# Hybrid decoder trunk in split f32: the places of matrix operands within 256 bytes of SBUF, and queries and keys computed with the weights stationary

## The chip, the cores and the metric

The kernel runs on one core of a Trainium2 chip. The metric is the device time in microseconds (us) of one execution. Three executions of the kernel before took 1136.25, 1136.45 and 1136.63 us, so the median is 1136.45 us. The profiled execution took 1136.86 us; the span from its first to its last instruction is 1135.1 us, so 1.76 us lie around the span.

## The reference

One sequence of 256 tokens with 2048 features passes one layer, all in f32:

```
h = rms_norm(x, norm1_g);  proj = h @ w_in                    # 2048 x 6152
q_a, k_a, v_a, f_a, q_b, k_b, v_b = split(proj)               # 8 + 8 heads of 128; f_a: 8 columns
y_a = forgetting attention(q_a, k_a, v_a, log_sigmoid(f_a + forget_b))
y_b = dilated attention(q_b, k_b, v_b, rel_bias)              # three dilations, mixed by their softmax sums
x = x + concat(rms_norm(y_a), rms_norm(y_b)) @ w_out          # 2048 x 2048
h = rms_norm(x, norm2_g)
x = x + square(relu(h @ w_mlp_in)) @ w_mlp_out                # 2048 x 8192, 8192 x 2048
out = rms_norm(x, final_norm_g)
```

## The kernel before, in words

**Products.** Every f32 matrix is held as two `float32r` parts, hi and lo, and each product is three: hi by hi, lo by hi, hi by lo. A matrix product on TensorE (PE) has a stationary operand of 128 by 128, which a weight load (LDWEIGHTS, the row PEld) brings in, and a moving operand that is streamed past it. The profile names a product `acc<-moving,stationary`.

**Chunks, steps, slots.** The weights are taken in chunks of 512 columns, in the order in which they run: for each of four groups of four heads `q`, `v`, `k` (16 feature tiles each), eight chunks `o` of `w_out` (8 tiles each), then four rounds of four chunks `u` (`w_mlp_in`) and four chunks `d` (`w_mlp_out`) of 16 tiles. A slot is one feature tile of 128 rows (`kt`), a step is two slots. SP loads the raw weights of two steps in one DMA. `split` (L144) makes the parts of a step three steps ahead: ScalarE (ACT) writes `whi` (L168), VectorE (DVE) writes `wlo` (L169). There are four buffers of each, so ACT starts on a step's `whi` when PE has done with the one four steps earlier.

**Two forms.** In the plain form (`product`, L295: q, k, v, o, d) the activations are stationary and 512 weight columns move: six products a slot. In the turned form (`turned_product`, L303: only u) the weights are stationary, in four blocks of 128 columns, and 256 tokens move: twelve products a slot. The plain form leaves tokens on the partitions, the turned form features.

**Accumulators.** A chunk has two PSUM tiles `acc`; the pool holds four, so a chunk needs the two that were freed by the chunk before the last. What empties them, and all the attention work, is tied to slots by `at(slot, function)` and written out behind that slot's products (`run_side`). Each engine works through its instructions in that written order.

**Queries and keys.** `drain_qk` empties q and k into `nat`, ACT one half, DVE the other, and scales rows by the norm of their token. `turn_qk` then turns each pair of heads with four PE transposes (L463) and splits the result from PSUM. `e` is the last slot of the chunk: drain at `e` (for the first chunk at `e + 3`), turning at `e + 2` and `e + 3`. Of the k chunk's attention, the last head's `values` comes at `e + 29`, which is slot `e + 13` of the next q chunk, and `group_norm` of the second group at `e + 31`, slot `e + 15` of the next q chunk.

**Places.** The start of a tile in a partition of SBUF, modulo 256 bytes, follows from the order and sizes of the tiles in the pools. By the addresses in the built programs it is:

| tile | before | after |
|---|---|---|
| `aT_hi`, `aT_lo` (normed x, features on partitions): stationary for q, k, v; moving for u | 224 | 32 |
| `big_hi`, `big_lo` (attention output, later the MLP's hidden state): stationary for o, d | 160 | 32 |
| `whi`, `wlo` where they move | 160 | 32 |
| `whi`, `wlo` where they are stationary | 160 | 224 |
| `q`, `v` parts: stationary in the attention | 224 | 0 |
| `k` and `p` (probability) parts: moving in the attention | 32 | 0 |

Rows of these tiles and the buffers of a pool are multiples of 256 bytes long, so each operand of a group starts at the same place. In the last d chunk the parts of its first four steps go into `aT_hi` and `aT_lo`, which are free then; there the moving operand starts at 224.

Of the kernel before, what the change touches and what calls it, by code (L numbers as in the profile page):

```python
# [19 lines left out]
P = 128  # L20
D_MODEL = 2048
SEQ = 256
# [15 lines left out]

LEAD = 3
WARM, WARM2 = 8, 1  # L40


def _constants():
    i = np.arange(P)
    upto = (i[:, None] <= i[None, :]).astype(np.float32)
    after = (i[:, None] > i[None, :]).astype(np.float32)
    tri = np.where(i[None, :] <= i[:, None], 0.0, NEG).astype(np.float32)
    head = (i[:, None] % 32 == np.arange(NH)[None, :]).astype(np.float32)
    pack = np.concatenate([after, -upto, tri, np.zeros((P, P), np.float32), tri, head], axis=1)
# [19 lines left out]
def kernel(  # L69
# [21 lines left out]
    w_in, w_out, w_up, w_down = w_in[0], w_out[0], w_mlp_in[0], w_mlp_out[0]  # L91

    one = ctx.enter_context(tc.tile_pool(name="one", bufs=1))
    two = ctx.enter_context(tc.tile_pool(name="two", bufs=2))
    wraw = ctx.enter_context(tc.tile_pool(name="wraw", bufs=4))
    wsplit = ctx.enter_context(tc.tile_pool(name="wsplit", bufs=LEAD + 1))
    psum = ctx.enter_context(tc.tile_pool(name="psum", bufs=2, space=PSUM))
    dram = ctx.enter_context(tc.tile_pool(name="dram", bufs=1, space=DRAM))
# [45 lines left out]
    def split(i, j0=0, n=2):  # L144
# [31 lines left out]
    warm = zeros[:, :CW // 2].bitcast(BF16)  # L176
    half_t = one.tile([P, TB], F32, name="half_t")
    ones = one.tile([P, 1], F32, name="ones")
    nc.vector.memset(zeros[:, :CW // 2], 0.0)
# [14 lines left out]
    for c in range(1, 4):  # L194
        load_x(4 * c, 4 * c + 4)
        load(2 * c)
    fb = one.tile([P, NH], F32, name="fb")
    relx = one.tile([N_BUCKETS + 1, NH], F32, name="relx")
    nc.vector.memset(relx, 1.0)
    pk = one.tile([P, 5 * P + NH], F32, name="pk")  # L200
    pick_sb = two.tile([P, RW], F32, name="pr")[:N_BUCKETS + 1]
# [8 lines left out]

    mcat = pk[:, 2 * P:5 * P]
    head = pk[:, 5 * P:]
    gcat = one.tile([P, TB, P], F32R, name="gcat")
# [8 lines left out]
    nc.scalar.activation(ones, ones, AF.Copy)  # L222
    gT = one.tile([P, 48], F32, name="gT")

# [30 lines left out]
    def rsqrt(dst, ssq, n):  # L255

        w = dst.shape[1]
        v = two.tile([P, TB], F32, name="rs_v")[:, :w]
        t = two.tile([P, TB], F32, name="rs_t")[:, :w]
# [7 lines left out]
    ssq1 = one.tile([P, TB, 4], F32, name="ssq1")  # L267
    ssq1s = one.tile([P, TB], F32, name="ssq1s")
    rstd1 = one.tile([P, TB], F32, name="rstd1")
    rstdq = one.tile([P, TB], F32, name="rstdq")  # L270

# [8 lines left out]
    def first_norm():  # L280
        nc.vector.tensor_reduce(ssq1s, ssq1, axis=mybir.AxisListType.X, op=ALU.add)
        rsqrt(rstd1, ssq1s, D_MODEL)
        nc.vector.tensor_scalar(rstdq, rstd1, QSCALE, None, op0=ALU.mult)

# [57 lines left out]

    logf = one.tile([P, TB, NH], F32, name="logf")
    lf_hi, lf_lo = (
# [12 lines left out]
    def forget_gates():  # L357
        f = psum.tile([P, 512], F32, name="tr")
        for t in range(TB):
            nc.tensor.transpose(f[:, 2 * t * NH:2 * (t + 1) * NH], fTs[0][:, t * P:(t + 1) * P], ident[:2 * NH, :2 * NH])  # L360
        z = one.tile([P, TB, NH], F32, name="fz")
        e = one.tile([P, TB, NH], F32, name="fe")
        u = one.tile([P, TB, NH], F32, name="fu")
        d = one.tile([P, TB, NH], F32, name="fd")
        n = one.tile([P, TB, NH], F32, name="fn")
        for t in range(TB):
# [76 lines left out]

    nat = {}

    def drain_qk(g, what, ci):
        acc = accs.pop(ci)
        scale = rstdq if what == "q" else rstd1
        ts = [two.tile([P, CW], F32, name="nat") for _ in range(TB)]
        nc.scalar.activation(ts[0], acc[0], AF.Copy, scale=scale[:, 0:1])  # L450
        nc.vector.tensor_scalar(ts[1], acc[1], scale[:, 1:2], None, op0=ALU.mult)
        nat[g, what] = ts

    def turn_qk(g, what, hp):
        ts = nat[g, what]
        if hp == 0:
# [7 lines left out]
        split_psum(  # L464
            th[:, 2 * hp:2 * hp + 2, :].rearrange("p h s -> p (h s)"),
            tl[:, 2 * hp:2 * hp + 2, :].rearrange("p h s -> p (h s)"), p,
        )
# [3 lines left out]
    def decay_of(hd):  # L471
        decay[hd] = two.tile([P, SEQ], F32R, name="gate_h")
        nc.gpsimd.tensor_scalar(
# [5 lines left out]
    def scores(g, h):  # L479
# [19 lines left out]
        pr = two.tile([P, 3 * P], F32, name="pr")  # L499
        st = two.tile([P, 3, TB], F32, name="st")  # L500
        for t, c0, c1 in spans:
            add = mcat[:, c0:c1] if kind == 0 else relT[:, hd, SEQ - (c1 - c0):]
            nc.vector.tensor_tensor_reduce(  # L503
# [25 lines left out]
    def values(g, h):  # L529
# [12 lines left out]
        first = seen[kind] == 0  # L542
        s = sq[kind] if first else two.tile([P, SEQ], F32, name="sqt")
        nc.scalar.activation(s, y[:, :SEQ], AF.Square)
# [4 lines left out]

    rstdo = [one.tile([P, TB], F32, name=f"rstdo{k}") for k in range(2)]  # L550

# [6 lines left out]

    ssq2 = one.tile([P, TB, 4], F32, name="ssq2")
    ssq2s = one.tile([P, TB], F32, name="ssq2s")  # L560
    rstd2 = one.tile([P, TB], F32, name="rstd2")
    rstd2sq = one.tile([P, TB], F32, name="rstd2sq")

# [30 lines left out]
    gf = relT.rearrange("p h s -> p (h s)")  # L594
    ssq3 = one.tile([P, TB, 5], F32, name="ssq3")
    ssq3s = one.tile([P, TB], F32, name="ssq3s")
    rstd3 = one.tile([P, TB], F32, name="rstd3")

# [31 lines left out]
    def finish(t, n, cs):  # L630
        r, s = rstd3[:, t:t + 1], ssq3s[:, t:t + 1]
        v = two.tile([P, 1], F32, name="fi_v")
        u = two.tile([P, 1], F32, name="fi_u")
        ru = two.tile([P, 1], F32, name="fi_ru")
        nc.vector.tensor_scalar(v, ssq3[:, t, n:n + 1], s, 1.0 / D_MODEL, op0=ALU.add, op1=ALU.mult)
# [39 lines left out]
    for ci, (what, key, *_rest) in enumerate(chunks[:-1]):  # L675
# [107 lines left out]
```

## Time and profile before

| what | value |
|---|---|
| median of three executions | 1136.45 us |
| profiled execution, its span | 1136.86 us, 1135.1 us |
| PE busy | 1124.0 us, 99% of the span |
| PE weight loads busy | 988.8 us, 87% |
| DVE, ACT, POOL busy | 56%, 46%, 3% |
| granted TensorE clock | 0.998 of full speed |
| HBM | 183 GB/s over the span |

Matmuls are pipelined: the profile's duration of one overlaps the next, so the cost of a product is read from the distance between starts, in the timeline or in the chain of waits, and not from its duration. The idle times of DVE and ACT cost nothing by themselves.

### The profile page before, as it was taken

The page shows a single profiled execution, that of the slowest core. Times are in us where ns is not written, and L with a number is a line of the kernel's source. Part 1 is how long each engine was busy: PE and PEld are TensorE (multiplying, and loading weights), DVE is VectorE, ACT ScalarE, POOL GpSimd, SP SyncE. Part 2 cuts the span into 40 slices and gives each one's busy share as a digit, 9 for nine tenths or more (in the row PEclk, how much of TensorE's full clock was granted, in tenths as well). Part 3 has the DMA queues.
Part 4 walks back from the last instruction along what each step waited for, and adds up shares of the span by engine and source line. Part 5 has one row for each costly group of instructions (what it writes and reads, how often), then busy time and mean ns, then how long its engine had stood idle before and what let it go on. Part 6 is the DMA issues. An engine that isn't in the chain of part 4 may idle for free.

```text
span 1135.1 us, 16038 instructions
## 1 busy us (share of the span) xinstructions
PE 1124.0 (99%) x6635; PEld 988.8 (87%) x6635; DVE 639.7 (56%) x795; ACT 521.9 (46%) x675; POOL 31.7 (3%) x57
## 2 busy tenths in 40 slices
PE   9999999999999999999999999999999999999996
PEld 6778888888888889998889998889998889999886
DVE  5665656556566665555555555545555554555564
ACT  5545545545445554454334444343544433454451
POOL 0100200100001000000000000000000000000000
PEclk9999999999999999999999999999999999999999
DMA  8655454454545556556555655566465566556642
GB/s 312 224 183 183 154 185 149 149 185 149 186 156 178 155 179 192 187 179 212 196 185 164 208 186 188 200 199 192 152 220 187 186 193 192 187 171 206 240 148 74
DMA packets 104933, 209.15 MB, mean 184 GB/s; under 512 B 3651, under 2 KB 4508, under 8 KB 104732
## 3 DMA queue, kind: packets, MB, share of 16 engines
q1 hardware_dynamic: 104556, 207.06, 55.8%
q0 software_dynamic: 304, 1.06, 0.3%
q8 instruction: 52, 0.85, 0.3%
q14 instruction: 21, 0.17, 0.0%
HBM read 206.00 MB, written 2.11 MB: 183 GB/s over the span
## 4 chain that ended last, share of the span: by engine, by line
PE 98%; DMA 1%; DVE 0%; SPq 0%; ACT 0%; POOL 0%; issue 0%; DVEq 0%
PE acc L313 32%; PE acc L299 21%; PE acc L301 21%; PE acc L300 21%; PE sc L493 1%; PE sc L538 1%; PE tr L463 1%; DMA raw<-in_w_in_dram 1%; PE tr L250 1%; PE tr L520 0%; PE sc L333 0%; PE sc L490 0%; DVE wlo L169 0%; ACT whi L168 0%; DVE xs L646 0%; SPq L185 0%
## 5 line engine op out<-in xcount | busy, mean ns | idle before, releaser
L169 DVE TENSOR_TENSOR wlo<-raw,whi 128x1024 fp32r<-128x1024 f32 (+1 forms) x381 | 464.1, 1224 | 374.4 <-ACT whi L168 371.6
L168 ACT ACTIVATE whi<-raw 128x1024 fp32r<-128x1024 f32 (+1 forms) x381 | 399.8, 1055 | 404.2 <-PE acc L300 241.4
L313 PE MATMUL acc<-aT_hi,whi 128*128 128x256 f32 x1024 | 287.2, 280 | 0.0
L313 PE MATMUL acc<-aT_hi,wlo 128*128 128x256 f32 x1024 | 286.1, 279 | 0.0
L313 PE MATMUL acc<-aT_lo,whi 128*128 128x256 f32 x1024 | 286.0, 279 | 0.0
L299 PE MATMUL acc<-whi,big_hi 128*128 128x512 f32 (+1 forms) x632 | 246.0, 389 | 0.0
L301 PE MATMUL acc<-wlo,big_hi 128*128 128x512 f32 (+1 forms) x632 | 244.7, 387 | 0.0
L300 PE MATMUL acc<-whi,big_lo 128*128 128x512 f32 (+1 forms) x632 | 244.5, 387 | 0.0
L313 PEld LDWEIGHTS acc<-aT_hi,wlo 128*128 128x128 f32 x1024 | 192.8, 188 | 0.0
L313 PEld LDWEIGHTS acc<-aT_hi,whi 128*128 128x128 f32 x1024 | 192.3, 188 | 0.2
L313 PEld LDWEIGHTS acc<-aT_lo,whi 128*128 128x128 f32 x1024 | 191.6, 187 | 0.2
L299 PE MATMUL acc<-whi,aT_hi 128*128 128x512 f32 x384 | 157.0, 409 | 0.0
L300 PE MATMUL acc<-whi,aT_lo 128*128 128x512 f32 x384 | 152.5, 397 | 0.0
L301 PE MATMUL acc<-wlo,aT_hi 128*128 128x512 f32 x384 | 152.3, 397 | 0.0
L301 PEld LDWEIGHTS acc<-wlo,big_hi 128*128 128x128 f32 x632 | 118.7, 188 | 24.4
L300 PEld LDWEIGHTS acc<-whi,big_lo 128*128 128x128 f32 x632 | 118.8, 188 | 23.4
L299 PEld LDWEIGHTS acc<-whi,big_hi 128*128 128x128 f32 x632 | 118.8, 188 | 22.9
L301 PEld LDWEIGHTS acc<-wlo,aT_hi 128*128 128x128 f32 x384 | 72.5, 189 | 17.4
L299 PEld LDWEIGHTS acc<-whi,aT_hi 128*128 128x128 f32 x384 | 72.7, 189 | 15.3 <-issue 0.6
L300 PEld LDWEIGHTS acc<-whi,aT_lo 128*128 128x128 f32 x384 | 72.7, 189 | 14.0 <-DVE aT_lo L240 0.2
L237 DVE TENSOR_TENSOR big_lo<-nat,big_hi 128x512 fp32r<-128x512 f32 x32 | 22.2, 693 | 22.3 <-ACT big_hi L236 22.3
L507 ACT ACTIVATE pr<-neg,st 128x128 f32<-128x128 f32 (+1 forms) x32 | 14.3, 448 | 40.8 <-DVE st L503 40.8
(160 smaller groups left out, 533.7 us busy)
## 6 DMA issues: line engine op xcount, KB each, us to landing
raw<-in_w_mlp_in_dram SPq DMA_DIRECT2D x64, 1024.0 KB, 5.3
raw<-in_w_mlp_out_dram SPq DMA_DIRECT2D x64, 1024.0 KB, 5.2
raw<-in_w_in_dram SPq DMA_DIRECT2D x42, 1024.0 KB, 5.2
raw<-in_w_out_dram SPq DMA_DIRECT2D x16, 1024.0 KB, 5.1
raw<-in_w_in_dram SPq DMA_DIRECT2D x4, 1040.0 KB, 5.3
raw<-in_w_in_dram SPq DMA_DIRECT2D x3, 512.0 KB, 8.6
xs<-in_x_dram SPq DMA_DIRECT2D x3, 512.0 KB, 9.6
big_lo<-rel_d POOLq DMA_DIRECT2D x1, 1024.0 KB, 7.3
```

Source lines behind the costliest of these rows:

```text
L168: nc.scalar.activation(hi, t, AF.Copy)
L169: nc.vector.tensor_tensor(lo, t, hi.bitcast(F32), op=ALU.subtract)
L237: nc.vector.tensor_tensor(lo, src, hi.bitcast(F32), op=ALU.subtract)
L250: nc.tensor.transpose(p[:, j * SEQ + t * P:j * SEQ + (t + 1) * P], xs[:, t, c:c + P], ident)
L299: nc.tensor.matmul(acc, xh, hi[:, j, cols], start=go, stop=False)
L300: nc.tensor.matmul(acc, xl, hi[:, j, cols], start=False, stop=False)
L301: nc.tensor.matmul(acc, xh, lo[:, j, cols], start=False, stop=end)
L313: nc.tensor.matmul(acc, w[:, j, b * P:(b + 1) * P], a[:, kt, :], start=kt == 0 and b % 2 == 0 and n == 0, stop=kt == kts - 1 and n == 2, s ...
L463: nc.tensor.transpose(p[:, j * SEQ + t * P:j * SEQ + (t + 1) * P], ts[t][:, h * P:(h + 1) * P], ident)
L493: nc.tensor.matmul(s[:, c0:c1], q[:, h, t * P:(t + 1) * P], k[:, h, :c1 - c0], start=n == 0 and kind == 1, stop=n == 2,)
L507: nc.scalar.activation(pr[:, c0:c1], neg[:, c0:c1], AF.Exp, bias=st[:, 0, t:t + 1], scale=-1.0, accum_out=st[:, 1, t:t + 1],)
L538: nc.tensor.matmul(y[:, o0:SEQ], v[:, t, h * P:(h + 1) * P], p[:, c0:c1], start=t == 0 and n == 0, stop=t == 1 and n == 2,)
```

## The change

Three things are changed.

The first is where tiles start. The pools are re-sorted (`lead_in`, `wide`, `few` are new), the parts of the weights get a buffer 256 bytes longer and start at 32 bytes in it where they move, or at 224 where they are stationary, and a tile of 32 bytes ahead of `aT_hi` puts all of `aT` and `big` at 32. To make room one zero block of the mask goes, and `gate_h` and `sqt` have one buffer in place of two.

The second is the form of q and k: they use the turned form, so they arrive with features on the partitions and the transposes go. Their scale now varies along the free axis, so a tile `rows1` with the tokens' factors on all partitions is made once, at slot 19, by two small DVE instructions and one f32 product (L465 of the new kernel). Each half of a chunk is emptied by one DVE instruction from PSUM (L474), then split from SBUF.

The third is when: queries are emptied at `e + 14` and `e + 15`, keys at `e` and `e + 1`.

```diff
+LINE, NEAR, FAR = 64, 8, 56
+TURNED = "qku"
...
-            hi, lo = (wsplit.tile([P, 2, CW], F32R, name=n) for n in ("whi", "wlo"))
+            b = FAR if chunks[ci][0] in TURNED else NEAR
+            hi, lo = (
+                wsplit.tile([P, 2 * CW + LINE], F32R, name=n)[:, b:b + 2 * CW].rearrange("p (j c) -> p j c", j=2)
+                for n in ("whi", "wlo")
+            )
...
-    aT_hi = one.tile([P, KT, SEQ], F32R, name="aT_hi")
-    aT_lo = one.tile([P, KT, SEQ], F32R, name="aT_lo")
+    wide.tile([P, NEAR], F32, name="ahead")
+    aT_hi = wide.tile([P, KT, SEQ], F32R, name="aT_hi")
+    aT_lo = wide.tile([P, KT, SEQ], F32R, name="aT_lo")
...
-        if what == "u":
+        if what in TURNED:
             return turned_product(ci, i, j, kt, kts)
...
-    yT_hi = one.tile([P, 2 * NH, SEQ], F32R, name="big_hi")
-    yT_lo = one.tile([P, 2 * NH, SEQ], F32R, name="big_lo")
+    yT_hi = wide.tile([P, 2 * NH, SEQ], F32R, name="big_hi")
+    yT_lo = wide.tile([P, 2 * NH, SEQ], F32R, name="big_lo")
...
+    def first_norm_rows():
+        d = two.tile([P, CW], F32, name="nat")
+        square = d[:, SEQ:SEQ + P]
+        nc.gpsimd.memset(square, 1.0)
+        p = psum.tile([P, 512], F32, name="tr")
+        for t in range(TB):
+            nc.vector.tensor_scalar(d[:, t * P:(t + 1) * P], ident, rstd1[:, t:t + 1], None, op0=ALU.mult)
+        nc.tensor.matmul(p[:, :SEQ], square, d[:, :SEQ], start=True, stop=True)
+        nc.scalar.activation(rows1, p[:, :SEQ], AF.Copy)
+
+    def drain_qk(g, what, ci, half):
+        if half == 0:
             qkv[g, what] = [one.tile([P, 4, SEQ], F32R, name=what + n) for n in ("_hi", "_lo")]
         th, tl = qkv[g, what]
-        p = psum.tile([P, 512], F32, name="tr")
-        for j in range(2):
-            for t in range(TB):
-                h = 2 * hp + j
-                nc.tensor.transpose(p[:, j * SEQ + t * P:j * SEQ + (t + 1) * P], ts[t][:, h * P:(h + 1) * P], ident)
+        acc = accs[ci][half]
+        n = two.tile([P, CW], F32, name="nat")
+        nc.vector.scalar_tensor_tensor(
+            n.rearrange("p (h s) -> p h s", h=2), acc.rearrange("p (h s) -> p h s", h=2),
+            QSCALE if what == "q" else 1.0, rows1[:, None, :].to_broadcast([P, 2, SEQ]),
+            op0=ALU.mult, op1=ALU.mult,
+        )
         split_psum(
...
-            late = 3 if ci == 0 else 0
-            at(e + late, drain_qk, key, what, ci)
-            at(e + late + 2, turn_qk, key, what, 0)
-            at(e + late + 3, turn_qk, key, what, 1)
+            late = 14 if what == "q" else 0
+            at(e + late, drain_qk, key, what, ci, 0)
+            at(e + late + 1, drain_qk, key, what, ci, 1)
...
+    at(19, first_norm_rows)
```

On PE, around an eviction of queries and keys before, the transposes stand between plain products. Here the scores of one head (L493) end, and the two turnings of a q chunk (L463) follow among the v chunk's products:

```order
L493 MATMUL sc<-k_hi,q_lo 128x256
L463 MATMUL tr<-ident,nat 128x128 x4
L299 MATMUL acc<-whi,aT_hi 128x512
L300 MATMUL acc<-whi,aT_lo 128x512
L301 MATMUL acc<-wlo,aT_hi 128x512
L299 MATMUL acc<-whi,aT_hi 128x512
L300 MATMUL acc<-whi,aT_lo 128x512
L301 MATMUL acc<-wlo,aT_hi 128x512
L463 MATMUL tr<-ident,nat 128x128 x4
```

In the changed kernel there is no such row. This is PE where the third group's v chunk ends (L310 to L312, plain) and its k chunk begins (L324, turned, one row a product); L570 belongs to `group_norm`:

```order
L570 MATMUL tr<-ones,sq_140 128x1 x2
L310 MATMUL acc<-whi,aT_hi 128x512
L311 MATMUL acc<-whi,aT_lo 128x512
L312 MATMUL acc<-wlo,aT_hi 128x512
L310 MATMUL acc<-whi,aT_hi 128x512
L311 MATMUL acc<-whi,aT_lo 128x512
L312 MATMUL acc<-wlo,aT_hi 128x512
L324 MATMUL acc<-aT_hi,whi 128x256
L324 MATMUL acc<-aT_lo,whi 128x256
L324 MATMUL acc<-aT_hi,wlo 128x256
```

The first L324 writes the accumulator of the q chunk's first half, the seventh that of its second half; each waits until DVE has emptied it.

The third place is DVE at the same point. Before, from the last values of the second group (`big_lo`) to the third group's v chunk being emptied (`v_lo`), with the five small instructions of `group_norm` (`rs_v`, `rs_t`, `rstdo`) between:

```order
L240 SCALAR_TENSOR_TENSOR big_lo<-sc,gT,big_hi 128x256
L169 TENSOR_TENSOR wlo<-raw,whi 128x1024
L260 TENSOR_SCALAR rs_v<-tr 128x2
L262 TENSOR_TENSOR rs_t<-rstdo_132 128x2
L263 TENSOR_TENSOR rs_t<-rs_t,rs_v 128x2
L264 TENSOR_SCALAR rs_t<-rs_t 128x2
L265 TENSOR_TENSOR rstdo_132<-rstdo_132,rs_t 128x2
L240 SCALAR_TENSOR_TENSOR v_lo<-acc,rstd_117,v_hi 128x512 x2
```

And after:

```order
L253 SCALAR_TENSOR_TENSOR big_lo<-sc,gT,big_hi 128x256
L474 SCALAR_TENSOR_TENSOR nat<-acc,rows_139 128x512
L250 TENSOR_TENSOR q_lo<-nat,q_hi 128x512
L181 TENSOR_TENSOR wlo<-raw,whi 128x1024
L273 TENSOR_SCALAR rs_v<-tr 128x2
L275 TENSOR_TENSOR rs_t<-rstdo_142 128x2
L276 TENSOR_TENSOR rs_t<-rs_t,rs_v 128x2
L277 TENSOR_SCALAR rs_t<-rs_t 128x2
L278 TENSOR_TENSOR rstdo_142<-rstdo_142,rs_t 128x2
L474 SCALAR_TENSOR_TENSOR nat<-acc,rows_139 128x512
L250 TENSOR_TENSOR q_lo<-nat,q_hi 128x512
L253 SCALAR_TENSOR_TENSOR v_lo<-acc,rstd_127,v_hi 128x512 x2
```

The two evictions of queries (L474) moved in here; the second stands behind a weight split and the group's norm. On ACT the first half's `q_hi` stands ahead of the next `whi`.

## Rows read from the trace of the kernel before

**Rows 1.** The page: span, busy times, and the chain that ended last.
```profile
span 1135.1 us, 16038 instructions
PE 1124.0 (99%) x6635; PEld 988.8 (87%) x6635; DVE 639.7 (56%) x795; ACT 521.9 (46%) x675; POOL 31.7 (3%) x57
PE 98%; DMA 1%; DVE 0%; SPq 0%; ACT 0%; POOL 0%; issue 0%; DVEq 0%
```

**Rows 2.** Chain of waits by time: start, us, what; first d round, second u round.
```profile
506.14 0.24 PE acc L299
593.22 90.45 PE acc L313 x768
683.67 0.24 PE acc L299
```

**Rows 3.** Timeline, PE (start, duration, instruction): fourth group's v chunk.
```profile
300.05 0.40 PE L299 MATMUL acc<-whi,aT_hi 128*128 128x512 f32 x1
...
315.45 0.40 PE L299 MATMUL acc<-whi,aT_hi 128*128 128x512 f32 x1
```

**Rows 4.** Timeline, PE: end of the last chunk, 256 columns moving.
```profile
1120.61 0.28 PE L299 MATMUL acc<-aT_hi,big_hi 128*128 128x256 f32 x1
...
1123.44 0.29 PE L299 MATMUL acc<-whi,big_hi 128*128 128x256 f32 x1
...
1125.96 0.28 PE L299 MATMUL acc<-whi,big_hi 128*128 128x256 f32 x1
```

**Rows 5.** Timeline, PE: values of two heads, first and fourth product.
```profile
282.59 0.28 PE L538 MATMUL sc<-p_hi,v_hi 128*128 128x256 f32 x1
...
282.93 0.22 PE L538 MATMUL sc<-p_hi,v_hi 128*128 128x128 f32 x1
...
343.15 0.28 PE L538 MATMUL sc<-p_hi,v_hi 128*128 128x256 f32 x1
...
343.51 0.22 PE L538 MATMUL sc<-p_hi,v_hi 128*128 128x128 f32 x1
```

**Rows 6.** Chain of waits by time: one turning of two heads.
```profile
89.67 0.44 PE tr L463 x4
```

**Rows 7.** Timeline, PE: the f32 product of 384 columns, and the next.
```profile
68.62 0.81 PE L416 MATMUL sc<-pr,relx 33*8 33x384 f32 x2
69.36 0.50 PE L299 MATMUL acc<-whi,aT_hi 128*128 128x512 f32 x1
```

**Rows 8.** Timeline: second group, last values, to the k chunk's first product.
```profile
136.94 0.38 ACT L544 ACTIVATE sqt<-sc 128x256 f32<-128x256 f32 x1 [1.26 <-PE sc L538]
137.73 0.48 DVE L240 SCALAR_TENSOR_TENSOR big_lo<-sc,gT,big_hi 128x256 fp32r<-128x256 f32 x1 [0.78 <-ACT big_hi L239]
140.94 0.39 PE L299 MATMUL acc<-whi,aT_hi 128*128 128x512 f32 x1
```

**Rows 9.** Timeline: the same in the third group, with `group_norm`.
```profile
214.34 0.48 DVE L240 SCALAR_TENSOR_TENSOR big_lo<-sc,gT,big_hi 128x256 fp32r<-128x256 f32 x1 [0.78 <-ACT big_hi L239]
216.95 0.15 DVE L260 TENSOR_SCALAR rs_v<-tr 128x2 f32<-128x2 f32 x1
217.19 0.73 POOL L261 TENSOR_TENSOR rstdo<-rs_v,half_t 128x2 f32<-128x2 f32 x1 [2.37 <-DVE rs_v L260]
218.00 0.40 PE L299 MATMUL acc<-whi,aT_hi 128*128 128x512 f32 x1
218.55 0.16 DVE L265 TENSOR_TENSOR rstdo<-rstdo,rs_t 128x2 f32<-128x2 f32 x1
```

**Rows 10.** Groups by line: names, shapes, count | busy us, mean ns | idle before.
```profile
L169 DVE TENSOR_TENSOR wlo<-raw,whi 128x1024 fp32r<-128x1024 f32 (+1 forms) x381 | 464.1, 1224 | 374.4 <-ACT whi L168 371.6
L168 ACT ACTIVATE whi<-raw 128x1024 fp32r<-128x1024 f32 (+1 forms) x381 | 399.8, 1055 | 404.2 <-PE acc L300 241.4 <-PE acc L313 154.8 <-DMA raw<-in_w_in_dram 4.6
L236 ACT ACTIVATE big_hi<-nat 128x512 fp32r<-128x512 f32 x32 | 20.2, 632 | 26.1 <-DVE nat L587 26.1
L568 DVE SCALAR_TENSOR_TENSOR xs<-acc,rstdo,xs 128x512 f32<-128x512 f32 x16 | 11.3, 745 | 0.0
```

More of the change, by code (lines that the diff above doesn't have):

```diff
@@ L48, in _constants @@
     head = (i[:, None] % 32 == np.arange(NH)[None, :]).astype(np.float32)
-    pack = np.concatenate([after, -upto, tri, np.zeros((P, P), np.float32), tri, head], axis=1)
+    pack = np.concatenate([after, -upto, np.zeros((P, P), np.float32), tri, head], axis=1)
     dist = np.arange(RW) - 127
@@ L176 @@
     warm = zeros[:, :CW // 2].bitcast(BF16)
-    half_t = one.tile([P, TB], F32, name="half_t")
-    ones = one.tile([P, 1], F32, name="ones")
+    half_t = few.tile([P, TB], F32, name="half_t")
+    ones = few.tile([P, 1], F32, name="ones")
     nc.vector.memset(zeros[:, :CW // 2], 0.0)
@@ L196 @@
         load(2 * c)
-    fb = one.tile([P, NH], F32, name="fb")
-    relx = one.tile([N_BUCKETS + 1, NH], F32, name="relx")
+    fb = few.tile([P, NH], F32, name="fb")
+    relx = few.tile([N_BUCKETS + 1, NH], F32, name="relx")
     nc.vector.memset(relx, 1.0)
-    pk = one.tile([P, 5 * P + NH], F32, name="pk")
+    pk = few.tile([P, 4 * P + NH], F32, name="pk")
     pick_sb = two.tile([P, RW], F32, name="pr")[:N_BUCKETS + 1]
@@ L222 @@
     nc.scalar.activation(ones, ones, AF.Copy)
-    gT = one.tile([P, 48], F32, name="gT")
+    gT = lead_in.tile([P, 96], F32, name="gT")[:, :48]
     def gains(k0, k1):
@@ L257, in rsqrt @@
         w = dst.shape[1]
-        v = two.tile([P, TB], F32, name="rs_v")[:, :w]
-        t = two.tile([P, TB], F32, name="rs_t")[:, :w]
+        v = few.tile([P, TB], F32, name="rs_v", bufs=2)[:, :w]
+        t = few.tile([P, TB], F32, name="rs_t", bufs=2)[:, :w]
         nc.vector.tensor_scalar(v, ssq, 1.0 / n, EPS, op0=ALU.mult, op1=ALU.add)
@@ L265, in rsqrt @@
         nc.vector.tensor_tensor(dst, dst, t, op=ALU.mult)
[L267 to L270, printed above, removed]
+    ssq1 = few.tile([P, TB, 4], F32, name="ssq1")
+    ssq1s = few.tile([P, TB], F32, name="ssq1s")
+    rstd1 = few.tile([P, TB], F32, name="rstd1")
     def first_squares(t, c):
@@ L282, in first_norm @@
         rsqrt(rstd1, ssq1s, D_MODEL)
-        nc.vector.tensor_scalar(rstdq, rstd1, QSCALE, None, op0=ALU.mult)
     accs = {}
@@ L340, in at @@
         side.setdefault(i, []).append((f, a))
-    logf = one.tile([P, TB, NH], F32, name="logf")
+    logf = few.tile([P, TB, NH], F32, name="logf")
     lf_hi, lf_lo = (
@@ L360, in forget_gates @@
             nc.tensor.transpose(f[:, 2 * t * NH:2 * (t + 1) * NH], fTs[0][:, t * P:(t + 1) * P], ident[:2 * NH, :2 * NH])
[L361 to L365, printed above, removed]
+        z = few.tile([P, TB, NH], F32, name="fz")
+        e = few.tile([P, TB, NH], F32, name="fe")
+        u = few.tile([P, TB, NH], F32, name="fu")
+        d = few.tile([P, TB, NH], F32, name="fd")
+        n = few.tile([P, TB, NH], F32, name="fn")
         for t in range(TB):
@@ L442, in drain_v @@
         qkv[g, "v"] = (vh, vl)
[L444 to L456, printed above, removed]
+    rows1 = one.tile([P, SEQ], F32, name="rows1")
+    def first_norm_rows():
[9 more added lines that the diff above has]
+        if half == 0:
             qkv[g, what] = [one.tile([P, 4, SEQ], F32R, name=what + n) for n in ("_hi", "_lo")]
         th, tl = qkv[g, what]
-        p = psum.tile([P, 512], F32, name="tr")
-        for j in range(2):
-            for t in range(TB):
-                h = 2 * hp + j
-                nc.tensor.transpose(p[:, j * SEQ + t * P:j * SEQ + (t + 1) * P], ts[t][:, h * P:(h + 1) * P], ident)
+        acc = accs[ci][half]
[5 more added lines that the diff above has]
+        )
         split_psum(
-            th[:, 2 * hp:2 * hp + 2, :].rearrange("p h s -> p (h s)"),
-            tl[:, 2 * hp:2 * hp + 2, :].rearrange("p h s -> p (h s)"), p,
+            th[:, 2 * half:2 * half + 2, :].rearrange("p h s -> p (h s)"),
+            tl[:, 2 * half:2 * half + 2, :].rearrange("p h s -> p (h s)"), n,
         )
@@ L471, in decay_of @@
     def decay_of(hd):
-        decay[hd] = two.tile([P, SEQ], F32R, name="gate_h")
+        decay[hd] = two.tile([P, SEQ], F32R, name="gate_h", bufs=1)
         nc.gpsimd.tensor_scalar(
@@ L542, in values @@
         first = seen[kind] == 0
-        s = sq[kind] if first else two.tile([P, SEQ], F32, name="sqt")
+        s = sq[kind] if first else two.tile([P, SEQ], F32, name="sqt", bufs=1)
         nc.scalar.activation(s, y[:, :SEQ], AF.Square)
@@ L548, in values @@
         seen[kind] += 1
-    rstdo = [one.tile([P, TB], F32, name=f"rstdo{k}") for k in range(2)]
+    rstdo = [few.tile([P, TB], F32, name=f"rstdo{k}") for k in range(2)]
     def group_norm(kind):
@@ L557, in group_norm @@
         rsqrt(rstdo[kind], p[:, :TB], D_GRP)
[L559 to L562, printed above, removed]
+    ssq2 = few.tile([P, TB, 4], F32, name="ssq2")
+    ssq2s = few.tile([P, TB], F32, name="ssq2s")
+    rstd2 = few.tile([P, TB], F32, name="rstd2")
+    rstd2sq = few.tile([P, TB], F32, name="rstd2sq")
     def drain_o(kind, c, ci):
@@ L594 @@
     gf = relT.rearrange("p h s -> p (h s)")
-    ssq3 = one.tile([P, TB, 5], F32, name="ssq3")
-    ssq3s = one.tile([P, TB], F32, name="ssq3s")
-    rstd3 = one.tile([P, TB], F32, name="rstd3")
+    ssq3 = few.tile([P, TB, 5], F32, name="ssq3")
+    ssq3s = few.tile([P, TB], F32, name="ssq3s")
+    rstd3 = few.tile([P, TB], F32, name="rstd3")
     def load_gf():
```

17 lines of the change are left out of this document (10 added, 7 removed).

## The prediction

> **What bounds the kernel now.** I read the page's busy times and its chain first. The reader is to see that TensorE (PE) is busy for 99% of the span and holds 98% of the chain that ended last, while DVE and ACT are half idle [rows 1]. So the time is a sum of PE's products, and a change is worth what it does to their number, to the distance between their starts, and to PE's waits. Next I read distances, in the chain by time and in PE's timeline.
>
> - Turned products of u: 768 in 90.45 us, 0.1178 us each [rows 2].
> - Plain products of d: from 506.14 to 593.22 there are 384, 0.2268 us each [rows 2].
> - Plain products of q, k and v: from 300.05 to 315.45 there are 66, 0.2333 us each [rows 3].
>
> The last two have one shape, but stand 6.5 ns apart. What differs is where their operands start in a line of 256 bytes: moving and stationary at 160 and 160 in d, at 160 and 224 in q, k, v. The last chunk shows it inside one stage and over one stationary tile: 24 products of 256 columns with the moving operand at 224 take 2.83 us, 0.1179 each, and the next 21 with it at 160 take 2.52 us, 0.1200 each [rows 4]. So places do matter, by some per cent.
>
> The Trainium skill speaks against this: its page "TensorE: Matmul & The Clock Gate", section "Step-by-step: what each phase is for", says that PE has two independent read ports into SBUF, and that loading the next weights takes no read bandwidth from the running product. By that rule places are free and the sum is that of the third rival below; the trace does not agree, since rows 4 differ by 2.1 ns at one shape.
>
> **The change part by part.** All sums are against the profiled execution, 1136.86 us (span 1135.1 us and 1.76 us around it); the median of the runs is 0.41 us below it, and I take that off at the end.
>
> *Transposes.* One turning of two heads is four transposes, 0.44 us in the chain [rows 6]. Eight chunks of q and k have two each, so 16 x 0.44 = 7.0 us go. They lie on PE, with nothing beside them.
>
> *The row factors.* One f32 product of 256 columns is added. The trace's f32 product of 384 columns took 0.74 us to the next start [rows 7], so this is 0.74 x 256/384 = 0.5 us. The two DVE instructions that feed it come a whole chunk before their result is used; if DVE is late there, PE waits some tenths of a us once.
>
> *q and k turned.* 768 plain products become 1536 turned ones with moving and stationary at 32 and 224. In the attention before, products of 256 columns stand at just these places. Three of them in a row take 0.34 us in one head and 0.36 us in another [rows 5]; the sixteen such triples lie between these two and average 0.346 us, 0.1153 each. Bounds are 0.113 and 0.120; I take 0.1153, the mean at the same places and width. 1536 x 0.1153 = 177.1 us replace 768 x 0.2333 = 179.2 us: -2.1 us.
>
> *u.* The same places and products: 3072 x (0.1153 - 0.1178) = -7.7 us.
>
> *v, o, d.* All become 32 and 32. No row has that for 512 columns. Nearest is d with 160 and 160, equal places too, at 0.2268. The largest difference that places make between rows of 512 columns is 6.5 ns, so I bound it by 0.2203 and 0.2333. With the moving operand at 32 the 256-column triples are 2 to 5 ns below those with it at 224 or 160 [rows 4, 5], so I lean below d and take 0.225. v has 384 products: 384 x (0.225 - 0.2333) = -3.2 us. o and d have 1848 that stream `whi` or `wlo` at full width: 1848 x (0.225 - 0.2268) = -3.3 us.
>
> *The evictions.* They leave ACT one copy less and give DVE one instruction more a chunk; both are half idle [rows 1], and their waits cost nothing as long as PE has its operands. Late queries change that. A k chunk writes the accumulators of the q chunk before it. Their second half is emptied at e + 15 and the k chunk begins at e + 17, two slots or 2.8 us later. In the second group DVE comes to it like this, with the mean durations by line [rows 10]: `big_lo` of the last values ends at 138.21 [rows 8]; first half emptied, 0.745, at 138.96; ACT's `q_hi`, 0.632, at 139.6; only then ACT's next `whi`, which stands behind it, 1.055, at 140.65; DVE's `wlo`, 1.224, at 141.9; second half, 0.745, at 142.6, with handovers some 142.7. PE's seventh product of the k chunk wants it at 140.94 [rows 8] + 6 x 0.118 = 141.65, or 141.5 with v faster. So PE waits 1.2 us, with every product behind it. The fourth group has the same queue: 1.2 us. In the third, `group_norm` stands ahead of the second half: `big_lo` ends at 214.82, and the same steps bring `wlo` to 218.5; from `rs_v` to the last `rstdo`, with POOL between, took 216.95 to 218.71, 1.76 us [rows 9]; so 220.25, and the eviction ends at 221.0, with handovers 221.1. PE wants it at 218.00 + 0.7 - 0.15 = 218.55: a wait of 2.5 us. The first group has no attention before it, and there the second half is emptied in time. Together +4.9 us, between 0 and 7. The weights are split three steps (8 us) ahead, so these waits go no further.
>
> *At no cost.* The single buffers of `gate_h` and `sqt` are used once in four slots, and POOL is 3% busy [rows 1]. SP issues the same weight loads in the same order; nothing is moved past a queue.
>
> Sum: -7.0 + 0.5 - 2.1 - 7.7 - 3.2 - 3.3 + 4.9 = -17.9 us, so 1119.0 for a profiled execution and **1118.5 us** for the median.
>
> **The rivals.**
>
> *Streams at 32 are faster than I take them.* If equal places at 32 reach the lower bound, 0.2203, v gives -5.0 and o and d -12.0 in place of -3.2 and -3.3: 1108 us; turned products at 0.113 as well would give 1097. For it: the best triples are at 0.113. Against: they are short sequences.
>
> *Only the distance between the two places counts.* It is 0 in d before and in all plain products after, and 64 in u before (224 and 160) and in the turned ones after (32 and 224, modulo 256). Then u, o and d stay, v falls to 0.2268 (-2.5), q and k cost 1536 x 0.1178 - 179.2 = +1.7, and -7.0 + 0.5 + 4.9 remain: -2.4, so 1134 us. For it: the change keeps both distances. Against: the attention at distance 64 averages 0.1153, not 0.1178.
>
> *Places do nothing; the stage does.* The slower rate of q, k, v would come from the attention and its traffic. Then only +1.7, -7.0, +0.5 and +4.9 count: 1136.5 us, no change. For it: rows 2 and 3 are of different stages. Against: rows 4. This is the time that the skill's two ports would give.
>
> *Slower: 32 with 32 is a bad pair.* If plain products there stand 0.2333 apart, as those of q, k, v do now, o and d cost 1848 x 0.0065 = 12.0 us more, v nothing less, and with turned products left at 0.1178 the sum is +12.1: 1148.5 us. It decides from a plain distance of 0.2279 on if turned products gain nothing, from 0.2330 on if they gain what I take. For it: no row shows the pair. Against: of the two plain pairs in rows 2 and 3 the one with equal places is the faster.
>
> **How the numbers follow.** The forecast has 52%, faster streams 17%, distance alone 16%, stage alone 7%, the bad pair 8%. The forecast's own range is 1110 to 1127, from turned products 2 ns either way. The range of 8 in 10 takes in most of the faster streams at its low end, and the two cases without a gain at its high end: 1103 to 1137 us. A measurement of this kernel can tell 0.2%, 2.3 us, from no change. Faster by more: the forecast (51), faster streams (17), over half of distance alone (9), 1 of the others: 78%. Within: 13%. Slower: 9%, the bad pair and late evictions on top of no gain.
>
> **What would show it.** In the profile after, each u round of 768 products should take 88.5 us in place of 90.45 and each d round 86.4 in place of 87.1; the v products should stand about 0.225 apart. No L463 should be left, and L324 should count 4608 products. At the start of the second, third and fourth k chunk PE should wait some 1.2, 2.5 and 1.2 us for DVE's L474, seven products in. Rounds of u and d with unchanged lengths would mean distance or stage; d rounds at 89 us and more would mean the bad pair. What makes the prediction wrong above all is the distance of plain products at 32 and 32, since each ns of it is 2.2 us.

## The result and the profile after

Four executions of the changed kernel took 1129.44 to 1132.04 us, median 1131.36, beside 1136.54 us for the kernel before on the same chip. The ratio is 0.995, its 95% interval 0.9933 to 0.9967: 0.5% faster. The forecast was 1118.5 us. The profiled execution took 1131.91 us, 4.95 less than that of before.

The page of the changed kernel, span and busy times, as in [rows 1]:

```profile
span 1130.1 us, 17447 instructions
PE 1116.1 (99%) x7341; PEld 1018.1 (90%) x7341; DVE 644.0 (57%) x804; ACT 517.1 (46%) x668; POOL 34.6 (3%) x58
```

PE is still what bounds it. The chain of waits by time (start, us, what), first and second round of u, the start of the first round of d, and the third round of u, against [rows 2]:

```profile
418.30 82.97 PE acc L324 x732
501.27 0.23 PE acc L310
...
588.33 90.45 PE acc L324 x768
765.83 90.45 PE acc L324 x768
```

The second and third rounds take 90.45 us to the hundredth, as before. The round of d, 501.27 to 588.33, takes 87.06 where it took 87.08. So neither moved with its places. The first round of u did: 82.97/732 = 0.1133 us a product. Before, it stood at 86.22/732 = 0.1178:

```profile
419.92 86.22 PE acc L313 x732
```

The same shape at the same places has two distances, and a whole round keeps one of them.

The other places are read from PE's timeline (start, duration, instruction). First the values of one head, for [rows 5], then the fourth group's v chunk behind it:

```profile
280.77 0.28 PE L553 MATMUL sc<-p_hi,v_hi 128*128 128x256 f32 x1
...
281.12 0.22 PE L553 MATMUL sc<-p_hi,v_hi 128*128 128x128 f32 x1
...
282.17 0.40 PE L310 MATMUL acc<-whi,aT_hi 128*128 128x512 f32 x1
...
283.56 0.40 PE L310 MATMUL acc<-whi,aT_hi 128*128 128x512 f32 x1
...
284.93 0.39 PE L310 MATMUL acc<-whi,aT_hi 128*128 128x512 f32 x1
...
286.29 0.39 PE L310 MATMUL acc<-whi,aT_hi 128*128 128x512 f32 x1
```

The triple takes 0.35 us, some 0.117 a product. In v, six products, from the fourth after the attention's on, take (283.56 - 282.17)/6 = 0.2317 us each, and six more, a few products on, (286.29 - 284.93)/6 = 0.2267, d's distance. ([rows 3] is headed v; it lies in the k chunk that follows, at the same places.) So v starts anew after each piece of attention, and gets the better rate here only a dozen products later.

The waits of PE for the evictions of queries, added up (total, times, longest):

```profile
PE acc L324 <- DVE nat L474: 3.0, 3, 1.8
```

The chain by time at the second group's k chunk, and below it the third group's with `group_norm`, for [rows 8, 9]:

```profile
134.67 0.48 DVE big_lo L253
135.16 0.61 DVE nat L474
...
136.32 1.06 ACT whi L180
...
137.41 1.22 DVE wlo L181
138.63 0.61 DVE nat L474
...
139.28 0.74 PE acc L324 x4
...
214.58 0.08 DVE rs_v L273
...
214.72 0.74 POOL rstdo L274
...
216.25 0.61 DVE nat L474
...
216.90 0.62 PE acc L324 x3
```

This is the queue that the prediction wrote out. The chain leaves PE here, runs through DVE, ACT's next `whi`, DVE's `wlo` and the second eviction, and comes back at PE's seventh product.

Where 4.95 us went, by adding up the distances from each PE start to the next by operation, over the whole timeline of either kernel:

| operation | before | after |
|---|---|---|
| u, 3072 products | 362.0 | 358.7 |
| v, 384 | 91.7 | 90.3 |
| q and k, 768 plain or 1536 turned | 184.0 | 188.9 |
| their transposes (64), the row factors | 5.9 | 0.2 |
| o and d | 437.9 | 437.7 |
| first products, waiting for DMA (L220, L232) | 4.4 | 5.1 |

These make 4.9 us less; the attention's own products give back 0.3, and the transposes of x take 0.4 less. q and k alone, with their transposes and PE's waits, gained only 0.7. No L463, the turning of [rows 6], is left.

### The profile page after: what moved, and what is told of

It is laid out like the page before. It is cut to its first block, busy times and chain, and to the rows that moved or that the text cites. A ratio compares the mean times of both kernels' runs of the same rounds, so it can differ in the third digit from the quotient of the medians.

```text
span 1130.1 us, 17447 instructions
## 1 busy us (share of the span) xinstructions
PE 1116.1 (99%) x7341; PEld 1018.1 (90%) x7341; DVE 644.0 (57%) x804; ACT 517.1 (46%) x668; POOL 34.6 (3%) x58
## 4 chain that ended last, share of the span: by engine, by line
PE 97%; DVE 1%; ACT 0%; DMA 0%; issue 0%; POOL 0%; SPq 0%; DVEq 0%; ACTq 0%
PE acc L324 48%; PE acc L310 15%; PE acc L311 15%; PE acc L312 15%; PE sc L508 1%; PE sc L553 1%; PE tr L263 1%; PE tr L535 0%; DMA grow<-in_norm_g_dram 0%; PE sc L344 0%; DVE wlo L181 0%; DVE nat L474 0%; ACT whi L180 0%; PE sc L505 0%; DVE big_lo L253 0%
## 5 line engine op out<-in xcount | busy, mean ns | idle before, releaser
L324 PE MATMUL acc<-aT_hi,whi 128*128 128x256 f32 x1536 | 431.3, 281 | 3.0 <-DVE nat L474 3.0
L324 PE MATMUL acc<-aT_hi,wlo 128*128 128x256 f32 x1536 | 429.9, 280 | 0.0
L324 PE MATMUL acc<-aT_lo,whi 128*128 128x256 f32 x1536 | 429.1, 279 | 0.0
L324 PEld LDWEIGHTS acc<-aT_hi,whi 128*128 128x128 f32 x1536 | 289.0, 188 | 5.0 <-DVE nat L474 3.6
L324 PEld LDWEIGHTS acc<-aT_lo,whi 128*128 128x128 f32 x1536 | 289.8, 189 | 0.5 <-DVE aT_lo L253 0.2
L324 PEld LDWEIGHTS acc<-aT_hi,wlo 128*128 128x128 f32 x1536 | 289.5, 188 | 0.0
L310 PE MATMUL acc<-whi,big_hi 128*128 128x512 f32 (+1 forms) x632 | 245.7, 389 | 0.0
L312 PE MATMUL acc<-wlo,big_hi 128*128 128x512 f32 (+1 forms) x632 | 244.4, 387 | 0.0
L312 PEld LDWEIGHTS acc<-wlo,big_hi 128*128 128x128 f32 x632 | 118.7, 188 | 24.3
L310 PEld LDWEIGHTS acc<-whi,big_hi 128*128 128x128 f32 x632 | 118.8, 188 | 23.3
L310 PE MATMUL acc<-whi,aT_hi 128*128 128x512 f32 x128 | 52.1, 407 | 0.0
L311 PE MATMUL acc<-whi,aT_lo 128*128 128x512 f32 x128 | 50.4, 394 | 0.0
L312 PE MATMUL acc<-wlo,aT_hi 128*128 128x512 f32 x128 | 50.0, 391 | 0.0
L312 PEld LDWEIGHTS acc<-wlo,aT_hi 128*128 128x128 f32 x128 | 24.1, 188 | 5.5
```

The costliest lines, as they stand in the source:

```text
L310: nc.tensor.matmul(acc, xh, hi[:, j, cols], start=go, stop=False)
L311: nc.tensor.matmul(acc, xl, hi[:, j, cols], start=False, stop=False)
L312: nc.tensor.matmul(acc, xh, lo[:, j, cols], start=False, stop=end)
L324: nc.tensor.matmul(acc, w[:, j, b * P:(b + 1) * P], a[:, kt, :], start=kt == 0 and b % 2 == 0 and n == 0, stop=kt == kts - 1 and n == 2, s ...
```

## The experiments

Theories: **distance** (a product's rate follows the difference between the two operands' places modulo 256 bytes, whatever the places are), **absolute** (32 is a good place), **stage** (places do nothing). Here and below, a distance in us or ns lies between the starts of two products; a bare one, such as distance 64, is the moving operand's place minus the stationary one's, in bytes modulo 256. Later, for the two distances of a turned product: **entry** (what PE runs just ahead of a stretch sets which it takes) against chance. The experiments ran on several chips, on which the kernel before had medians of 1136.5 to 1138.1 us. Each ratio is against the kernel before on the same chip; what sets two experiments apart is read from their traces.

**One: the places without the form.**

```diff
-TURNED = "qku"
+TURNED = "u"
...
+        nc.scalar.activation(ts[0], acc[0], AF.Copy, scale=scale[:, 0:1])
+        nc.vector.tensor_scalar(ts[1], acc[1], scale[:, 1:2], None, op0=ALU.mult)
...
+                nc.tensor.transpose(p[:, j * SEQ + t * P:j * SEQ + (t + 1) * P], ts[t][:, h * P:(h + 1) * P], ident)
```

> The places of the change (32 and 224) with queries and keys as they were: plain products, drained by ACT and DVE, transposed on PE. All plain products have both operands at 32, u has them at 32 and 224. Distance theory (a product's rate follows the distance between the two places, modulo 256): q, k and v, 1152 plain products, go from 0.2333 to 0.2268 us, -7.5 us; o and d stay; u stays or, round by round, gains up to 3.4 us: 1129 us, 1126 at the least, some 2 us faster than the changed kernel. Absolute theory (the gain hangs on the turned products at 32): u alone moves. Stage theory (the rate of q, k, v comes from the attention beside them): q, k, v stay at 0.2333 and the time at 1136.

Measured 1128.73 us (1128.08 to 1129.49), ratio 0.9925 (0.9913 to 0.9938): 2.6 us below the changed kernel. The timeline of PE in the fourth k chunk, 90 products from the first row to the second:

```profile
291.05 0.39 PE L312 MATMUL acc<-whi,aT_hi 128*128 128x512 f32 x1
...
311.45 0.39 PE L312 MATMUL acc<-whi,aT_hi 128*128 128x512 f32 x1
```

20.40/90 = 0.2267 us, against 0.2333 in [rows 3]: the same stage, DMA and engines, other places. The stage theory falls. The total agrees with the expected one, its parts less well: the sums by operation give q, k and v 4.4 us less, not 7.5, as many of their short stretches beside attention stay at 0.230 and more; most of the rest is the first round of u, at 82.97 us here too.

**Two: the form without the places.** The kernel before with queries and keys turned, evicted and timed as in the changed kernel.

```diff
-        if what == "u":
+        if what in "qku":
...
+            late = 14 if what == "q" else 0
+            at(e + late, drain_qk, key, what, ci, 0)
+            at(e + late + 1, drain_qk, key, what, ci, 1)
```

> The places of before with queries and keys turned and the queries evicted 14 slots later. Turned products have 224 and 160, o and d 160 and 160, v 160 and 224. Distance theory: -7.0 for the transposes, +0.5 for the row factors, 1536 x 0.1178 - 768 x 0.2333 = +1.7, +3.5 for PE's waits at three k chunks, so -1.3: 1135 us; v stays at 0.2333 apart. If the turned products of q and k find the faster of their two distances (0.1133 in place of 0.1178 us) in part, down to 1131. If the changed kernel's gain is one of the turned form and not of the places: 1131.

Measured 1135.65 us, ratio 0.9986 (0.9977 to 0.9995): 1.3 us below before. Evicted as late as this, the form is worth next to nothing, as the distance theory has it; PE's waits at the three k chunks are in that, 3.3 us by its timeline (0.69, 1.93, 0.71). The chain shows its first round of u, at 224 and 160:

```profile
417.24 86.22 PE acc L313 x732
```

That is 0.1178, where the changed kernel has 0.1133, at one and the same distance between the places, 64.

**Three: queries four slots earlier.**

```diff
-            late = 14 if what == "q" else 0
+            late = 10 if what == "q" else 0
```

> The changed kernel with the queries evicted 10 slots later in place of 14. Theory that PE's waits at the second to fourth k chunk (0.75, 1.95 and 0.75 us) come from the second half being emptied too late: it is emptied four slots, 6.7 us, earlier, the waits go, and the time falls by up to 3.5 us to 1128. Rival: DVE and ACT are then behind with other work (the splits of weights or the normalisation of the attention's output), and PE waits there as long: 1131.

Measured 1127.03 us (1126.02 to 1127.78), ratio 0.991 (0.9897 to 0.9924), 4.3 below the changed kernel. The page's group of the product that waited (line, operation, shapes, count | busy us, mean ns | idle before), and the chain at the second k chunk:

```profile
L324 PE MATMUL acc<-aT_hi,whi 128*128 128x256 f32 x1536 | 430.3, 280 | 0.0
```

```profile
138.39 31.09 PE acc L324 x264
```

The waits are gone and turned up nowhere else: 264 products run through. They were 3.45 of the 4.3 us; of the rest, 0.55 is an earlier start, which the change of slots does not touch (PE's first turned product begins at 6.82 us in place of 7.37). With that, the turned form is 1.7 us better than the plain one of the first experiment; with 14 slots it was 2.6 worse.

**Four: all pairs of places, alone.** The computation is left out but for products; for 8 by 8 places:

```python
for om in range(0, 64, 8):          # moving, in floats: 32-byte steps
    for os in range(0, 64, 8):      # stationary
        plain(om, os)               # 36 products of 512 columns
        turned(om, os)              # 72 of 256
        transposes()                # 4
        turned(om, os)
```

> Measures the disputed cost by itself; the whole computation is left out but for the products. For each of 8 places of the moving operand (0 to 224 in a 256-byte line, in steps of 32) and 8 of the stationary one, PE runs 36 plain products (512 columns), 72 turned ones (256 columns), 4 transposes and 72 turned ones again, with nothing else going on. Distance theory: the mean distance of products in a cell depends on moving minus stationary modulo 256 alone: plain about 0.227 at equal places and 0.233 at 192 (160 and 224); turned 0.118 or 0.113 at 64, 0.120 at 192. Absolute theory: cells on one diagonal differ, and 32 with 32 or 32 with 224 stand out. No effect of places: all cells alike, 0.227 and 0.118. If the faster of the turned distances (0.113) is a matter of place, it fills some cells wholly; if of what runs before, it changes between the two stretches of one cell.

Mean distances (ns), from a stretch's third product on, by moving minus stationary, modulo 256; each from eight pairs of places, with how many pairs or stretches where they differ:

| distance | plain | turned, 16 stretches |
|---|---|---|
| 0 | 226.7 (7), 227.6 | 120.0 |
| 32 | 233.3 | 116.7 (13), 117.8 (3) |
| 64 | 228.9 (7), 233.3 | 113.3 (8), 117.8 (8) |
| 96 | 233.3 to 233.6 | 120.0 |
| 128 | 232.4 to 233.5 | 118.7 |
| 160 | 233.9 to 234.4 | 117.3 (12), 118.7 (4) |
| 192 | 233.3 | 113.3 (9), 117.8 (7) |
| 224 | 233.0 | 118.3 |

Three cells in the chain by time: 32 with 32 (from 313.87); the changed kernel's pair, 32 with 224 (from 468.85); and 64 with 0, another pair at distance 64 (from 494.17):

```profile
313.87 8.17 PE plain L77 x36
322.04 8.63 PE turned L86 x72
...
468.85 8.24 PE plain L77 x36
477.09 8.17 PE turned L86 x72
485.26 0.44 PE tr L93 x4
485.69 8.48 PE turned L86 x72
494.17 8.24 PE plain L77 x36
502.41 8.48 PE turned L86 x72
```

For the rates only the difference counts: of the eight pairs at one distance at least seven agree within half a nanosecond nearly everywhere, and 32 is no better than 160. Every kernel row fits: q, k, v before (160 and 224, distance 192) 233.3; o and d (0) 226.7 before and after; the end of the last chunk [rows 4] 117.9 at distance 64 and 120.0 at 0. With nothing else running the stage has no part in it. Which of 113.3 and 117.8 a stretch takes is not settled by its pair of places: the cell of 32 with 224 has one, then, after four transposes, the other (8.17 and 8.48 us for 72). But place may have a part in it. With plain products at the pair's own places just ahead, the first stretch at distance 64 has 113.3 at five pairs and 117.8 at three; the last row above is one of those.

**Five: distance 32 in place of 64,** in the kernel of the third experiment.

```diff
-LINE, NEAR, FAR = 64, 8, 56
+LINE, NEAR, FAR = 64, 8, 64
```

> The kernel with queries 10 slots late, its turned weights moved on by 32 bytes, from 224 to 0: turned products have moving and stationary at 32 and 0, distance 32 in place of 64, nothing else is touched. From the map of places: distance 32 runs at 116.7 ns (in 3 of 16 stretches at 117.8) and never at 113.3. If that map holds in the kernel, the three rounds of u at 117.78 fall by 768 x 1.1 ns = 0.85 us each, q and k by 1536 x 1.1 = 1.7, and the first round of u, at 113.45 before, rises by 2.4: 1127.0 - 2.6 - 1.7 + 2.4 = 1125.1 us. If places do not carry over from the map to a kernel with traffic: 1127. If the slower of the two distances is taken throughout: 1130.4.

Measured 1126.44 us (1126.01 to 1127.02), ratio 0.9909 (0.9892 to 0.9925). By time alone this can't be told from the third experiment. The chain can tell: first, second and third round of u.

```profile
412.64 85.40 PE acc L324 x732
...
585.10 89.60 PE acc L324 x768
...
761.77 89.60 PE acc L324 x768
```

89.60/768 = 0.1167 in the later rounds and 85.40/732 = 0.1167 in the first, which lost its 0.1133: both as the map has it for distance 32. The profiled spans are 1.2 us apart (1125.6 and 1124.4) and the medians 0.6, where 1.9 was expected: by the sums, q and k gave 1.5 of the 1.7 us forecast for them and u 0.1 of 0.2, and other transposes and the first products took 0.3 more.

**Six: what sets the two distances, alone.** 36 plain products at 32 and 32, an entry, 72 turned ones at 32 and 224.

> What sets which of its two distances (113.3 or 117.8 ns) a stretch of turned products at 32 and 224 runs at? The computation is left out but for products: 36 plain products at 32 and 32, then one of 30 entries (nothing; 1 to 4 transposes; one product of 16 to 240 columns; two or three of them; turned products and transposes as at the start of the first round of u), then 72 turned products; each entry four times, in four orders. Theory that the entry sets it: the four stretches behind one entry agree, nothing as an entry gives 117.8 as in the later rounds of u, and some entries give 113.3. Rival, that it is chance or something outside PE: stretches behind one entry disagree, about as often as those behind different ones.

The chain by time, with one to three transposes (L92) as entries:

```profile
91.80 8.48 PE turned L85 x72
...
108.45 0.11 PE tr L92
108.56 8.48 PE turned L85 x72
...
125.21 0.22 PE tr L92 x2
125.43 8.17 PE turned L85 x72
...
141.78 0.33 PE tr L92 x3
142.11 8.48 PE turned L85 x72
```

Of 30 entries 28 gave the same in all four orders: 27 always 117.8, one always 113.3. With nothing ahead: 117.8, four of four. One product of 16 to 240 columns, or two or three: always 117.8. Two transposes: 113.3 in three of four. The entry that the first round of u has (24 turned products, four transposes, 12, four): 113.3 in four of four. So with nothing else running the entry decides for 28 of 30; the other two (two transposes, and 24 turned products with four transposes, 113.3 in one of four) gave both, so something else has a part. What stands further ahead counts too: here 117.8 comes straight behind plain products at 32 and 32, in the map 113.3 behind plain ones at 32 and 224.

**Seven and eight: entries in the kernel.** Idle transposes of the identity are put ahead of the later rounds of u, in the kernel of the third experiment: two of them, or the whole entry of the first round (the two comments name the experiment).

```diff
+def ENTRY(what, key, kt):
+    return 2 if what == "u" and key[0] and key[1] == 0 and kt == 0 else 0           # seven
+    return 4 if what == "u" and key[0] and key[1] == 0 and kt in (2, 3) else 0      # eight
...
+        for m in range(ENTRY(chunks[ci][0], chunks[ci][1], kt)):
+            if m == 0:
+                p = psum.tile([P, 512], F32, name="tr")
+            nc.tensor.transpose(p[:, m * P:(m + 1) * P], ident, ident)
```

> The kernel with queries 10 slots late, and two transposes of the identity on PE, read by nobody, ahead of the second, third and fourth round of u. Theory that the instructions just ahead of a stretch set its distance, and that two transposes give the faster one (three of four stretches did, measured alone): each round of 768 falls from 117.78 to 113.33 ns a product, 3.41 us, less 0.14 for the transposes: -9.8 us, 1117.2. If one or two of the three rounds stay slow: 1120.5 or 1124. If the entry does not carry over into a kernel with traffic, or needs the place of the transposed block (128 there, 0 here): 1127.4, the transposes' 0.4 us more.

> The same kernel with the entry of its first round of u copied into the other three: 24 turned products, four transposes, 12 products, four transposes, and then the rest, all transposes of the identity and read by nobody. That entry gave 113.3 ns in four of four stretches measured alone and in the first round of u here. Theory: the other rounds fall by 732 x 4.45 ns = 3.26 us each, less twice 0.44 for the transposes: -7.1 us, 1119.9. If the entry does not decide: +2.6, 1129.7.

Seven: 1120.59 us, ratio 0.985 (0.9835 to 0.9864). Eight: 1120.52 us, 0.9847 (0.9832 to 0.9862). The rounds of u in the chain, first of seven, then of eight:

```profile
412.64 82.97 PE acc L333 x732
582.89 90.45 PE acc L333 x768
760.61 87.05 PE acc L333 x768
934.94 87.05 PE acc L333 x768
```

```profile
412.29 82.97 PE acc L333 x732
587.44 82.97 PE acc L333 x732
762.60 82.97 PE acc L333 x732
937.75 82.97 PE acc L333 x732
```

Two transposes win two rounds of three; the first round's entry wins all three. Instructions whose result nobody reads make the kernel some 6.5 us faster than the third experiment's. By the sums of the traces u gives 6.6 us in seven and 9.2 in eight, and the transposes take 0.4 and 2.1 of it back. Another 1.2 us come from the third k chunk and the start of the q chunk behind it, ahead of which nothing was put: first the third experiment, then eight.

```profile
214.15 31.09 PE acc L324 x264
213.88 29.92 PE acc L333 x264
```

That is 0.1178 and 0.1133; seven has 29.92 as well. Up to this chunk PE runs the same instructions in the same order in all three kernels, so in the kernel that order alone does not decide the distance. What else does was not tested.

**Nine: the same ahead of k chunks.**

```diff
+    return 2 if what == "k" and key and kt == 0 else 0
```

> Two transposes ahead of the second to fourth round of u, and also ahead of the second to fourth k chunk, which like u follow plain products and run at 117.8 ns for 264, 264 and 192 products. Theory as with u alone: 720 x 4.45 ns = 3.2 us, less 0.4 for three pairs, beyond u's: 2.8 us less than with the rounds of u alone, 1114.4. If the entry decides in u but attention's work beside k disturbs it: as with u alone or up to 0.4 more, 1117.6.

Measured 1121.04 us, ratio 0.9854 (0.9837 to 0.987), no better than seven. A miss: the second k chunk stayed slow, the third, fast in seven without an entry, is slow with one (the first row of the chain here), and only the fourth came down, while one round of u stayed slow as in seven.

```profile
214.70 31.09 PE acc L335 x264
289.01 21.77 PE acc L335 x192
```

**Ten: together.** The kernel of eight, with the weights of q and k at distance 32.

```diff
-            b = FAR if chunks[ci][0] in TURNED else NEAR
+            b = {"u": FAR, "q": LINE, "k": LINE}.get(chunks[ci][0], NEAR)
```

> What the runs point to, together: queries 10 slots late, the entry of the first round of u ahead of every round, u's weights at 224 (distance 64, held at 113.3 ns by its entry), and the weights of q and k at 0 (distance 32, 116.7 ns whatever comes before). Against the kernel with that entry alone, q and k gain 1.1 ns on those of their 1536 products that run at 117.8: 1.7 us less at the most, 1118.8; 0.6 less if as many of them run at 113.3 there as in its profiled run, 1119.9. If places and entry disturb each other (other products ahead of the first round of u), its round falls back to 117.8: 1123.

Measured 1119.68 us (1119.41 to 1120.05), ratio 0.9842 (0.9829 to 0.9855), the fastest median of all, though not to be told from eight by its interval. All rounds of u stayed at 82.97 us for 732. The new places of q and k are not shown to gain anything: their sums are 183.7 us here and 183.4 in eight, whose third k chunk stood at 0.1133; here it stands at 0.1178, which the map has at distance 32 too.

## Why the prediction was wrong, point by point

*What bounds the kernel* held: PE's distances and waits make up the whole difference.

*u, the step that failed first.* It was given 0.1153 for 0.1178, the mean of sixteen triples in the attention [rows 5]. That was a mean over two groups: ten triples at 0.114 and six at 0.117, near the two distances of the map, and none at 0.1153. The distance between the places allows both, and u already stood at 64. Measured: one round in four at 0.1133 and three unchanged, -3.3 us for -7.7. Two thirds of the whole gain are thus one round that changed over, which nothing in the prediction foresaw: that the time fell as far as it did is in good part luck.

*v, o, d.* They were lowered below 0.2268 because triples with the moving operand at 32 were faster than others. That read an absolute place where a distance was at work: o and d stay at distance 0 and at their time (-0.1 us, not -3.3). v does go from distance 192 to 0, but gains 1.4 us and not 3.2, nor the 2.5 of the rival: it is cut up by attention, and the rate comes back only after up to a dozen products.

*q and k turned.* Given -2.1; as far as can be told from the sums it was 188.9 - 184.0 = +4.9, of which 3.45 are the waits, so +1.5. The rival on distance said +1.7. Their transposes cost 5.9 us by their own distances, where 7.0 was forecast with the slower restart of the product behind them.

*The evictions.* The mechanism was right in every step, the size a little high: 1.2, 2.5 and 1.2 us forecast. From the start of the product due (0.12 us after the one before it) to the one that runs, the timeline gives 0.75, 1.95 and 0.75, 3.45 us in all. The largest part of the excess is the eviction, twice in the queue: taken at 0.745 us from [rows 10], where the chain has 0.61 for L474 (it lasts 0.68, but begins beside the instruction ahead of it). `q_hi`, taken at 0.632, let ACT's `whi` begin after 0.53. Experiment three shows that these waits were avoidable, and that taking them away cost nothing.

*The rivals.* "Only the distance counts", given 16% and 1134 us, was the right mechanism for the rates. Its missing 2.6 us are the first round of u (3.3), the smaller waits (1.45) and some 0.4 of small terms, against which stand 1.1 less on v, 0.9 less on transposes and row factors, and 0.6 at the start, where the first products wait longer for a DMA (in the third experiment, with the same start, that is gone). The argument against it, the attention's mean at distance 64, was the two distances again.

The rule on two independent read ports, weighed in the prediction from the Trainium skill's page "TensorE: Matmul & The Clock Gate" (section "Step-by-step: what each phase is for"), would, read as the prediction reads it, make every cell of the map alike; the map has 226.7 to 234.4 and 113.3 to 120.0 with nothing but PE running, so the measurement decides against it here.

*What stays open.* Why a place costs what it does; why a turned product at distance 64 or 192 has two distances; and what picks one. The entry is a part of the answer and not all of it: two transposes fail in some rounds, the same entry leads to 0.1178 before and in experiment two, where both places are others at the same difference, and the third k chunk has both distances behind one order of instructions. Such stretches may also be why the changed kernel's executions spread over 2.6 us; that was not shown, since only one of them has a trace.

## What to carry to other kernels

Before lowering a duration, ask what two groups of rows have in common beside the thing that changes: the fast and the slow pairs here differed in place and in distance, and for the rate only the distance counted; a small map of all pairs, run alone, settles that in one execution. A mean over short pieces can hide two values, so look at the single distances before it is carried to a long stretch. And where an eviction is moved close to the next write of its buffer, write out its engine's queue with what stands ahead of it on the other engines: that gave each wait to within 0.6 us.

## What the hardware showed that was not expected

- At a granted clock of 1.0 (2.4 GHz) 113.3 ns are 272 cycles for 256 columns, 117.8 some 283, 120.0 are 288; 226.7 and 233.3 ns are 544 and 560 for 512. What places cost is 16 cycles or so a product.
- A stretch of up to 768 products keeps its distance until something interrupts it: no round of u in any trace changed over in its last 732 products.
- In the kernel, plain products at equal places need up to a dozen after an interruption until they stand 0.2267 apart (0.2317 first); in the map, behind turned products, seven of eight stretches stood so from the third product on.
- Eight transposes whose output nobody reads, 0.88 us a round, make a round of u so much faster that the next begins 175.2 us after it (587.44 to 762.60 in eight) in place of 177.5 (588.33 to 765.83 in the changed kernel).
